# A gated three-branch decoder layer on one core: pools padded to 256 bytes, head outputs split by ScalarE and VectorE

## The chip, the core and the metric

The kernel runs on one core of a Trainium2 chip. Its engines are TensorE (matmuls, with the load of the stationary operand shown apart as PEld), VectorE (DVE), ScalarE (ACT), GpSimd (POOL) and SyncE (SP), which here only issues DMAs. The metric is the device time of one execution in microseconds, the median of three runs.

## The reference

One decoder layer on 512 tokens of width 1,024, in float32:

```
h = rmsnorm(x);  P = h @ w_in
A = gelu(g_rnn) * rg_lru(causal_conv4(x_rnn))            # 1024 wide
B = rmsnorm_per_head(diff_attention(dq, dk, dv)) * 0.8   # 4 heads of 128
C = forgetting_attention(fq, fk, fv, log_f)              # 8 heads of 64
m = sum_b sigmoid(gate_b) * (Y_b @ W_branch_b)           # Y_b = A, B, C
x = x + m @ w_out
x = x + geglu_with_causal_conv3(rmsnorm(x) @ ffn_up) @ ffn_down   # d_ff 2816
out = rmsnorm(x)
```

## The kernel before

**Arithmetic.** Every large matmul is done in three. Each float32 operand is split into a high part, rounded to TensorE's float32r, and a low part, the rest; then high x high, high x low and low x high are summed in PSUM. A split costs a copy or scaled copy on one engine (high) and a subtraction on another (low). `load_w` (L93) loads a weight tile on SP's DMA queue into `wr`, ScalarE writes `wh` (L101), VectorE `wl` (L102). `mm3` (L79) issues the three matmuls of each of 8 slices of the contraction, 24 for a tile of 512 columns; all of them are recorded at L77.

**Stages, in order of time.** Values of the diff heads (psv); then a list of units (L791 to L836): each unit is one attention head, `diff_head` (L439) or `fox_head` (L517), between whose pieces projections (psq, psk), the recurrent branch (psx, psg), the gates (psgt) and the branch products (psbr) are emitted as filler, by weights written out by hand. Then the output projection (pswo), the up projection with its convolution (psu), the down projection (psd). The order on each engine's queue is set when the program is scheduled, from this list.

**Head outputs.** A diff head ends with a scaled copy from PSUM into `yd` (L502); the four tiles are split much later by `ysplit` (L678), with ScalarE's copy (L682) and GpSimd's subtraction (L683), as an item of the unit of the first Fox head (`yds`, L797). Two Fox heads write the halves of one `yf` tile (L566, L567); the four tiles are split by the same helper in `end_attention` (L822). The recurrent branch's output `yr` goes through `ysplit` too. The branch products (`prod`, L655) read the parts.

**Space.** The pools lie one behind the other in each partition's bytes. Tiles are rounded up to 32 bytes. The constants end, and the page pool begins, at byte 23,840 = 93 x 256 + 32: 58 tiles of 2,048 bytes, which hold nearly everything 128x512, the parts of x and h2 that stream through TensorE among it. Behind it `wpool`: nine slots of 1,056 x 4 = 4,224 bytes, three each of `wr`, `wh` and `wl`; the three `wh` start at 160, 32 and 160 mod 256 and the three `wl` at 32, 160 and 32. Then the small tiles (`sm`, 3,008 bytes) and the 22 attention tiles of 2,048 bytes, at 96 mod 256, whose space takes ten pairs of `wo` and then of the FFN's activations (`act`, k < 10) later. Weight tiles take the three slots in turn.

**PSUM.** Four banks for the projections and products (`bank`, L67), four for attention (`abank`, L70). A projection's bank is free when VectorE has read it, as `xs` (L587) does for psx.

Of the kernel before, what the change touches and what calls it, by code (L numbers as in the profile page):

```python
# [24 lines left out]
NPG = 58  # L25
NAT = 22
NWARM = 9
NLAST = (2, 4)
LAM_INIT = 0.2
GELU_C = 0.7978845608028654  # L30
# [7 lines left out]
    COFF[_n] = _o  # L38
    _o += _w
NCOL = _o  # L40
ROFF = {"fbf": 0, "lam": 8}
NROW = 264

T_XR, T_GR, T_DQ, T_DK, T_FQ, T_FK, T_GT = 0, 8, 16, 20, 24, 28, 32

# [1 line left out]
def build(ctx, tc, A, out):  # L47
# [13 lines left out]
    def pg(name, dt=F32):  # L61
        return page.tile([128, 512], dt, name=name, tag="pg")

    def ag(name, dt=F32):
        return apool[0].tile([128, 512], dt, name=name, tag="at")
# [7 lines left out]
    def small(shape, name, bufs=None):  # L73
        return sm.tile(shape, F32, name=name, tag=name, bufs=bufs)
# [16 lines left out]
    hp = [False]  # L91

    def load_w(ap, n, parts=1):  # L93
        raw = wpool.tile([128, 1056], F32, name="wr", tag="wr")
        hi = wpool.tile([128, 1056], F32R, name="wh", tag="wh", bufs=3)
        lo = wpool.tile([128, 1056], F32R, name="wl", tag="wl", bufs=3)
        with tc.high_priority() if hp[0] else ExitStack():
            for p in range(parts):
                c = slice(n // parts * p, n // parts * (p + 1))
                nc.sync.dma_start(raw[:, c], ap[:, c])  # L100
                SC.copy(hi[:, c], raw[:, c])  # L101
                V.tensor_sub(lo[:, c], raw[:, c], hi[:, c])  # L102
        return hi, lo

    def load_wp(ap):

        raw = wpool.tile([128, 1056], F32, name="wr", tag="wr")
        nc.sync.dma_start(raw[:, :1024], ap)
        res = []
        for p in range(2):  # L110
            c = slice(512 * p, 512 * (p + 1))
            h = pg("wph", F32R)
            l = pg("wpl", F32R)
            SC.copy(h, raw[:, c])
            V.tensor_sub(l, raw[:, c], h)
            res.append((h, l))
        return res
# [39 lines left out]
    V.memset(epsc, EPS)  # L157
    pre = const.tile([128, 1], F32, name="pre")
    SC.activation(pre, epsc, AF.Exp)
    rows = const.tile([128, NROW], F32, name="rows")  # L160

    def col(n, j, w=1):
        return cols[:, COFF[n] + j:COFF[n] + j + w]
# [59 lines left out]
    nc.sync.dma_start(flip, A["flip"])  # L223
    flr = const.tile([128, 128], F32R, name="flr")
    V.tensor_copy(flr, flip)
    nc.sync.dma_start(rows, A["rows"].partition_broadcast(128))
    relb = const.tile([32, 4], F32, name="relb")
    nc.sync.dma_start(relb, A["rel_bias"])
    oh = ag("oh")[0:32, :]
# [19 lines left out]
    PE.matmul(bps[0:4, :], relb, oh, start=True, stop=True)  # L249
    bsb = ag("bsb")[0:4, :]  # L250
    V.tensor_copy(bsb, bps[0:4, :])
    bneg = const.tile([4, 128], F32, name="bneg")
    V.memset(bneg, NEG)
    bdr = dram.tile([4, 640], F32, name="bdr")
    nc.sync.dma_start(bdr[:, 0:512], bsb)
# [19 lines left out]
    def ev_fv(g):  # L275
        def ev(t, ps):
            p = pg("fv", F32R)

            pv = p.rearrange("p (u x d) -> p u x d", u=2, x=4)
            src = ps[:, 0:256].rearrange("p (u x d) -> p u x d", u=2, x=2)  # L280
            with tc.high_priority():
                for x in range(2):
                    h = pv[:, :, 3 * x, :]
                    l = pv[:, :, 1 + x, :]
                    SC.activation(h, src[:, :, x, :], AF.Copy, scale=rs1[:, t:t + 1])
                    V.scalar_tensor_tensor(l, src[:, :, x, :], rs1[:, t:t + 1], h, op0=MUL, op1=SUB)
            fv[t][g] = p
            if g == 0:
                V.scalar_tensor_tensor(flog[:, t, :], ps[:, 256:264], rs1[:, t:t + 1],
                                       rows[:, ROFF["fbf"]:ROFF["fbf"] + 8], op0=MUL, op1=ADD)  # L290
        return ev


# [13 lines left out]
        slabs.append(tl)  # L307


    lamw = rows[:, ROFF["lam"]:ROFF["lam"] + 256].rearrange("p (a b) -> p a b", a=4)  # L310
    lamp = ag("lamp")[:, 0:128].rearrange("p (a b) -> p a b", a=2)
    V.tensor_mul(lamp, lamw[:, 0::2, :], lamw[:, 1::2, :])
    lams = small([128, 2], "lams", 1)
    V.tensor_reduce(lams, lamp, axis=mybir.AxisListType.X, op=ADD)
    lame = small([128, 2], "lame", 1)
    SC.activation(lame, lams, AF.Exp)
# [122 lines left out]
    def diff_head(h, res):  # L439
        ws = []  # L440
        for i in range(NT):
            n = 128 * (i + 1)
            p = []
            nm = small([128, 2], "nm")
            mx = small([128, 2], "mx")
            sm_ = small([128, 2], "sum")
            for m in range(2):
                ps = scores(("d", h), m, i)
                sc = ag("sc")
                V.tensor_tensor_reduce(sc[:, :n], ps[:, :n], slabs[h][:, 512 - n:], 1.0, NEG, ADD, MAX,  # L450
                                       mx[:, m:m + 1])
                p.append(sc)
            V.tensor_scalar(nm, mx, -1.0, None, op0=MUL)
            for m in range(2):
                SC.activation(p[m][:, :n], p[m][:, :n], AF.Exp, bias=nm[:, m:m + 1], accum_out=sm_[:, m:m + 1])
            rc = small([128, 2], "rc")
            V.reciprocal(rc, sm_)
            V.tensor_mul(rc[:, 1:2], rc[:, 1:2], nlam)
            V.tensor_scalar(p[0][:, :n], p[0][:, :n], rc[:, 0:1], None, op0=MUL)
            V.scalar_tensor_tensor(p[0][:, :n], p[1][:, :n], rc[:, 1:2], p[0][:, :n], op0=MUL, op1=ADD)  # L460
            ws.append(p[0])
            yield
        yield "B"
        po = abank("pso")
        hs = slice(128 * h, 128 * (h + 1))

        def av(j):
            wh, wl = wt[j]
            c = slice(min(128 * j, 256), 512)
            for x, (a, b) in enumerate(((dvl[j][:, hs], wh), (dvh[j][:, hs], wl), (dvh[j][:, hs], wh))):  # L470
                mm(po[:, c], a, b[:, c], j == 0 and x == 0, j == NT - 1 and x == 2)

        wt = []
        for j in range(NT):
            wt.append(transposed(ws, j))
            if j:
                av(j - 1)
            if j % 2:
                yield
        av(NT - 1)  # L480
        o = ag("o")
        SC.copy(o, po)
        yield
        pt = abank("psq")
        for t in range(NT):
            PE.transpose(pt[:, 128 * t:128 * (t + 1)], o[:, 128 * t:128 * (t + 1)], ident)
        sq = ag("sq")
        so = small([128, NT], "so")
        for t in range(NT):
            c = slice(128 * t, 128 * (t + 1))  # L490
            SC.activation(sq[:, c], pt[:, c], AF.Square, accum_out=so[:, t:t + 1])
        rs = rsqrt_col(so, NT, "rso", 1.0 / 128)
        on = ag("on")
        for t in range(NT):
            c = slice(128 * t, 128 * (t + 1))
            V.tensor_scalar(on[:, c], pt[:, c], rs[:, t:t + 1], None, op0=MUL)
        yield
        pn = abank("psn")
        for t in range(NT):
            PE.transpose(pn[:, 128 * t:128 * (t + 1)], on[:, 128 * t:128 * (t + 1)], ident)  # L500
        y = pg("yd")
        SC.activation(y, pn, AF.Copy, scale=sg8)  # L502
        res.append(y)
        yield

    fo = {}
# [10 lines left out]
    def fox_head(hd, res):  # L517
# [48 lines left out]
        SC.copy(tmp[a], po[b])  # L566
        V.tensor_add(o[a], po[a], tmp[a])  # L567
        if m == 1:
            res.append(o)
        yield  # L570


# [105 lines left out]
    def ysplit(ys, name):  # L678
        for j in range(len(ys)):
            h = pg(name + "h", F32R)  # L680
            l = pg(name + "l", F32R)
            SC.copy(h, ys[j])  # L682
            G.tensor_sub(l, ys[j], h)  # L683
            ys[j] = (h, l)
# [62 lines left out]
    def do(f):  # L747
        return [(0.1, None, f)]
# [3 lines left out]
    def unit(gen, items):  # L752

        start = len(queue)
        queue.extend(items)
        plan.append((gen, start, len(queue)))
# [25 lines left out]
    def ckl(hd):  # L782
        return do(lambda: ck_load(hd))
# [3 lines left out]
    p1 = [f for c in range(0, 8, 2) for f in pi_(1, c)]  # L787
    vf = [(10, vload_t(A["wv_f0"], 4, 264), lambda w: vchunk_t(w, 4, 264, ev_fv(0))),
          (10, vload_t(A["wv_f1"], 4, 256), lambda w: vchunk_t(w, 4, 256, ev_fv(1)))]
    yds, yrs = do(lambda: ysplit(yd, "yd")), do(lambda: ysplit(yr, "yr"))  # L790
    unit(None, qi("d", 0) + ri(0))  # L791
    unit(DH(0, yd), qi("d", 1)[:1] + ri(1)[:1] + qi("d", 1)[1:] + ri(1)[1:] + re((0, 1)) + ri(2))
    unit(DH(1, yd), qi("d", 2)[:1] + gi(1, 1) + ri(3)[:1] + qi("d", 2)[1:] + ri(3)[1:])
    unit(DH(2, yd), gi(1, 0) + qi("f", 0)[:1] + qi("d", 3) + ri(4) + gi(1, 3))
    unit(DH(3, yd), vf[1:] + re((2, 3)) + vf[:1] + gi(1, 2) + gi(1, 4) + do(fox_prep) + qi("f", 0)[1:] + gi(1, 5)
         + gi(1, 6) + gi(1, 7) + qi("f", 1)[:1] + ckl(0))
    unit(F(0, yf), ri(5) + yds + ckl(1) + re((4, 5)))  # L797
    unit(F(1, yf), qi("f", 1)[1:] + ckl(2) + ri(6) + qi("f", 2)[:1])
    unit(F(2, yf), p1[2:] + p1[:1] + ri(7)[:1] + p1[1:2] + ri(7)[1:] + ckl(3))
    unit(F(3, yf), gi(0, 1) + gi(0, 0) + re((6, 7)) + yrs + ckl(4) + qi("f", 2)[1:] + gi(0, 2) + pi_(0, 1))  # L800
# [5 lines left out]
    wo = [None] * KD  # L806

    def wo_load(k):
        raw = wpool.tile([128, 1056], F32, name="wr", tag="wr")
        nc.sync.dma_start(raw[:, :1024], A["w_out"][128 * k:128 * (k + 1), :])  # L810
        hl = []
        for hf in range(2):
            al = ag if k < 5 else pg
            h = al("woh", F32R)
            l = al("wol", F32R)
            SC.copy(h, raw[:, 512 * hf:512 * (hf + 1)])
            V.tensor_sub(l, raw[:, 512 * hf:512 * (hf + 1)], h)
            hl.append((h, l))
        wo[k] = hl

    def end_attention():
        ysplit(yf, "yf")  # L822
        att_ctx.close()
        apool[0] = ctx.enter_context(tc.tile_pool(name="fpool", bufs=NAT))

# [67 lines left out]
                V.scalar_tensor_tensor(h2l[k][:, ts_], src, col("g2", k), h2h[k][:, ts_], op0=MUL, op1=SUB)  # L893


    fwh = const.tile([128, 88], F32, name="fwh")
    for j in range(3):
        V.tensor_scalar(fwh[:, 22 * j:22 * (j + 1)], col("fw", 44 * j + 22, 22), 0.5, None, op0=MUL)
    V.tensor_scalar(fwh[:, 66:88], col("fb", 22, 22), 0.5, None, op0=MUL)
# [166 lines left out]
```

## Time and profile before

| | |
|---|---|
| median of 3 runs | 949.76 us (948.43 to 950.57) |
| profiled execution | 949.56 us, its span 947.7 us |
| mean granted TensorE clock | 0.996 |
| busy: PE, DVE, ACT, POOL | 99%, 67%, 51%, 12% |
| matmuls | 4,363 |

The span runs from the first to the last instruction; 1.8 us of the profiled execution lie around it. A matmul's own duration (about 0.39 us at 512 columns) includes its way through the array, which the next one overlaps: what it costs is the time from its start to the next start. PEclk is the granted clock as a share of full speed (2.4 GHz); its lower level is 0.5.

### The profile page before, as it was taken

How to read it: one execution, taken by the hardware profiler on the slowest of the kernel's cores; microseconds unless marked ns; L12 is line 12 of the kernel's file. 1: busy time of each engine (PE TensorE's matmuls, PEld its weight loads, DVE VectorE, ACT ScalarE, POOL GpSimd, SP SyncE). 2: the span in 40 equal slices, each digit the busy share in tenths (PEclk: the TensorE clock that was granted, in tenths of full speed). 3: DMA queues.
4: the chain of work that ended last, by engine and by line, in shares of the span. 5: the costliest groups of instructions: out<-in, count | busy, mean ns of one | idle time of the engine just before them, and what ended most of it. 6: DMA issues, size and time to landing. Idle time of an engine off the chain costs nothing.

```text
span 947.7 us, 11817 instructions
## 1 busy us (share of the span) xinstructions
PE 934.7 (99%) x4363; PEld 770.7 (81%) x4363; DVE 631.7 (67%) x1207; ACT 486.6 (51%) x839; POOL 112.4 (12%) x85
## 2 busy tenths in 40 slices
PE   9999999999998999999999999999999999999997
PEld 6788888998886887888888889888888888888885
DVE  5779787777669889755566634877677677633323
ACT  7668776855474775434453344544444444422212
POOL 0022210200133253221210000000000000000000
PEclk9999999999999999999999999999999999999999
DMA  9622222232231323223253600323223222334112
GB/s 320 194 80 87 95 73 68 68 112 76 98 106 58 104 67 112 85 82 101 67 200 110 207 16 1 112 91 109 90 89 99 102 89 90 112 105 140 45 67 89
DMA packets 31433, 95.14 MB, mean 100 GB/s; under 512 B 3680, under 2 KB 5220, under 8 KB 31376
## 3 DMA queue, kind: packets, MB, share of 16 engines
q1 hardware_dynamic: 30800, 93.35, 29.2%
q10 hardware_dynamic: 576, 1.05, 0.3%
q8 instruction: 34, 0.56, 0.2%
q14 instruction: 23, 0.19, 0.1%
HBM read 92.26 MB, written 2.12 MB: 100 GB/s over the span
## 4 chain that ended last, share of the span: by engine, by line
PE 95%; DVE 3%; issue 1%; DMA 0%; ACT 0%; SPq 0%; POOLq 0%; POOL 0%
PE psu L77 26%; PE psgt L77 13%; PE psd L77 12%; PE psbr L77 9%; PE psg L77 6%; PE psv L77 5%; PE psx L77 5%; PE pswo L77 5%; PE psq L77 4%; PE psk L77 4%; PE pss L77 2%; PE pso L77 2%; PE pst L429 1%; DVE hh L637 1%; DVE gr L638 1%
## 5 line engine op out<-in xcount | busy, mean ns | idle before, releaser
L101 ACT CAST wh<-wr 128x1024 fp32r<-128x1024 f32 (+2 forms) x143 | 146.4, 1024 | 157.0 <-PE psu L77 55.3
L102 DVE TENSOR_TENSOR wl<-wr,wh 128x1024 fp32r<-128x1024 f32 (+2 forms) x143 | 174.1, 1217 | 75.3 <-ACT wh L101 66.7
L77 PE MATMUL psu<-h2l,wh 128*128 128x512 f32 (+1 forms) x360 | 136.9, 384 | 0.0
L77 PE MATMUL psu<-h2h,wh 128*128 128x512 f32 (+1 forms) x360 | 136.9, 383 | 0.0
L77 PE MATMUL psu<-h2h,wl 128*128 128x512 f32 (+1 forms) x360 | 87.2, 384 | 0.0
L77 PEld LDWEIGHTS psu<-h2l,wh 128*128 128x128 f32 x360 | 67.8, 188 | 14.0
L77 PEld LDWEIGHTS psu<-h2h,wh 128*128 128x128 f32 x360 | 67.8, 188 | 13.8
L77 PEld LDWEIGHTS psu<-h2h,wl 128*128 128x128 f32 x360 | 65.8, 188 | 14.4
L77 PE MATMUL psgt<-xh,wh 128*128 128x512 f32 x192 | 76.6, 399 | 0.0
L77 PE MATMUL psgt<-xl,wh 128*128 128x512 f32 x192 | 76.2, 397 | 0.0
L77 PE MATMUL psd<-wh,actl 128*128 128x512 f32 x128 | 50.2, 393 | 0.0
L77 PE MATMUL psd<-wl,acth 128*128 128x512 f32 x128 | 50.1, 391 | 0.0
L77 PE MATMUL psd<-wh,acth 128*128 128x512 f32 x128 | 49.9, 392 | 0.0
L77 PE MATMUL psgt<-xh,wl 128*128 128x512 f32 x192 | 49.1, 395 | 0.0
L864 POOL TENSOR_TENSOR rs3y<-rs3y,mhalf 128x1 f32<-128x1 f32 x4 | 2.2, 551 | 364.5 <-DVE rs3y L863 364.5
L77 PEld LDWEIGHTS psgt<-xh,wl 128*128 128x128 f32 x192 | 35.7, 188 | 8.1
L77 PEld LDWEIGHTS psgt<-xh,wh 128*128 128x128 f32 x192 | 36.1, 188 | 7.5
L77 PEld LDWEIGHTS psgt<-xl,wh 128*128 128x128 f32 x192 | 36.1, 188 | 7.5
L926 DVE SCALAR_TENSOR_TENSOR u<-gq,u 128x512 f32<-128x512 f32 x22 | 15.2, 692 | 34.1 <-ACT gq L925 34.1
L651 DVE TENSOR_TENSOR z<-psgt,rsb 128x512 f32<-128x512 f32 x24 | 16.5, 688 | 31.1 <-PE psgt L77 31.1
L906 DVE SCALAR_TENSOR_TENSOR u<-psu,cols,u 128x511 f32<-128x511 f32 (+1 forms) x44 | 32.9, 748 | 6.1 <-ACT u L903 5.3
L123 ACT CAST acth<-u 128x512 fp32r<-128x512 f32 x22 | 13.7, 621 | 43.5 <-DVE u L927 43.5
(288 smaller groups left out, 2179.6 us busy)
## 6 DMA issues: line engine op xcount, KB each, us to landing
wr<-w_t_in SPq DMA_DIRECT2D x56, 512.0 KB, 3.3
wr<-up_t_in SPq DMA_DIRECT2D x44, 512.0 KB, 3.3
wr<-dn_t_in SPq DMA_DIRECT2D x22, 512.0 KB, 3.4
wr<-br_r_in SPq DMA_DIRECT2D x8, 512.0 KB, 3.4
wr<-w_out_in SPq DMA_DIRECT2D x8, 512.0 KB, 3.9
xraw<-xT_in SPq DMA_DIRECT2D x8, 256.0 KB, 6.0
wr<-wv_d_in SPq DMA_DIRECT2D x8, 256.0 KB, 5.4
xt<-x_in SPq DMA_DIRECT2D x8, 256.0 KB, 5.4
```

The costliest lines, as they stand in the source:

```text
L77: PE.matmul(ps, a, b, start=start, stop=stop)
L101: SC.copy(hi[:, c], raw[:, c])
L102: V.tensor_sub(lo[:, c], raw[:, c], hi[:, c])
L123: SC.copy(h, src)
L429: PE.transpose(ps[:, 128 * i:128 * (i + 1)], ws[i][:, 128 * j:128 * (j + 1)], ident)
L637: V.tensor_tensor_scan(hh, a, xc, 0.0, op0=MUL, op1=ADD)
L638: V.scalar_tensor_tensor(gr, gr, 0.5, hh, op0=MUL, op1=MUL)
L651: V.tensor_mul(z, ps, rsb)
L864: G.tensor_tensor(y, y, mhalf[:, 0:1], op=ALU.pow)
L906: V.scalar_tensor_tensor(u[:, s:], ps[:, :512 - s], w[j], u[:, s:], op0=MUL, op1=ADD)
L926: V.scalar_tensor_tensor(ug, q, 1.0, ug, op0=ADD, op1=MUL)
```

## The change

Two things are done. First, sizes are changed so that each pool's start and slots are multiples of 256 bytes: the weight slots get 1,088 columns instead of 1,056 (4,352 bytes, 17 x 256); the constants lose the vectors for lambda (`rows`, from 264 columns to 8) and `bneg`, both now in one attention tile `lamr`, and `fwh` grows from 88 to 144 columns: 1,024 + 512 - 224 = 1,312 bytes less, so the page pool begins at 22,528 = 88 x 256. `lams` grows by 64 bytes, so the small tiles take 3,072. The load of `rows` becomes two DMAs. Second, `diff_head` writes the high part straight from PSUM (ScalarE) and the low part from PSUM (VectorE); `fox_head` calls `split` (L119: ScalarE copy, VectorE subtraction) on each finished `yf`; the calls of `ysplit` for yd and yf go. The one for yr stays.

```diff
+WCOL = 1088
...
-ROFF = {"fbf": 0, "lam": 8}
-NROW = 264
+NFB = 8
...
-        raw = wpool.tile([128, 1056], F32, name="wr", tag="wr")
-        hi = wpool.tile([128, 1056], F32R, name="wh", tag="wh", bufs=3)
-        lo = wpool.tile([128, 1056], F32R, name="wl", tag="wl", bufs=3)
+        raw = wpool.tile([128, WCOL], F32, name="wr", tag="wr")
+        hi = wpool.tile([128, WCOL], F32R, name="wh", tag="wh", bufs=3)
+        lo = wpool.tile([128, WCOL], F32R, name="wl", tag="wl", bufs=3)
...
-    rows = const.tile([128, NROW], F32, name="rows")
+    rows = const.tile([128, NFB], F32, name="rows")
...
-    nc.sync.dma_start(rows, A["rows"].partition_broadcast(128))
+    nc.sync.dma_start(rows, A["rows"][0:NFB].partition_broadcast(128))
+    lamr = ag("lamr")
+    nc.sync.dma_start(lamr[:, 0:256], A["rows"][NFB:NFB + 256].partition_broadcast(128))
...
-    bneg = const.tile([4, 128], F32, name="bneg")
+    bneg = lamr[0:4, 384:512]
...
-    lamw = rows[:, ROFF["lam"]:ROFF["lam"] + 256].rearrange("p (a b) -> p a b", a=4)
-    lamp = ag("lamp")[:, 0:128].rearrange("p (a b) -> p a b", a=2)
+    lamw = lamr[:, 0:256].rearrange("p (a b) -> p a b", a=4)
+    lamp = lamr[:, 256:384].rearrange("p (a b) -> p a b", a=2)
     V.tensor_mul(lamp, lamw[:, 0::2, :], lamw[:, 1::2, :])
-    lams = small([128, 2], "lams", 1)
+    lams = small([128, 24], "lams", 1)[:, 0:2]
...
-        y = pg("yd")
-        SC.activation(y, pn, AF.Copy, scale=sg8)
-        res.append(y)
+        h = pg("ydh", F32R)
+        l = pg("ydl", F32R)
+        SC.activation(h, pn, AF.Copy, scale=sg8)
+        V.scalar_tensor_tensor(l, pn, sg8, h, op0=MUL, op1=SUB)
+        res.append((h, l))
...
         if m == 1:
-            res.append(o)
+            res.append(split(o, "yf"))
...
-    yds, yrs = do(lambda: ysplit(yd, "yd")), do(lambda: ysplit(yr, "yr"))
+    yrs = do(lambda: ysplit(yr, "yr"))
...
-    unit(F(0, yf), ri(5) + yds + ckl(1) + re((4, 5)))
+    unit(F(0, yf), ri(5) + ckl(1) + re((4, 5)))
...
     def end_attention():
-        ysplit(yf, "yf")
...
-    fwh = const.tile([128, 88], F32, name="fwh")
+    fwh = const.tile([128, 144], F32, name="fwh")
```

## Rows read from the trace of the kernel before

**Rows 1.** The page: busy shares (part 1), and the chain that ended last (part 4).

```profile
PE 934.7 (99%) x4363; PEld 770.7 (81%) x4363; DVE 631.7 (67%) x1207; ACT 486.6 (51%) x839; POOL 112.4 (12%) x85
...
PE 95%; DVE 3%; issue 1%; DMA 0%; ACT 0%; SPq 0%; POOLq 0%; POOL 0%
```

**Rows 2.** The chain in order of time: start, length, what, and matmuls in it.

```profile
505.54 22.15 PE psbr L77 x96
...
574.49 5.50 PE psu L77 x46
580.86 239.11 PE psu L77 x1082
819.97 115.79 PE psd L77 x504
```

**Rows 3.** Timeline of TensorE, up projection, two weight tiles: start, duration, what.

```profile
658.90 0.40 PE L77 MATMUL psu<-h2h,wh 128*128 128x512 f32 x1
...
662.40 0.40 PE L77 MATMUL psu<-h2l,wh 128*128 128x512 f32 x1
662.64 2.02 PE L77 MATMUL psu<-h2h,wl 128*128 128x512 f32 x8
664.50 0.39 PE L77 MATMUL psu<-h2h,wh 128*128 128x512 f32 x1
...
667.90 0.40 PE L77 MATMUL psu<-h2l,wh 128*128 128x512 f32 x1
```

**Rows 4.** The same view of the down projection's last tiles, all in pages.

```profile
922.89 0.39 PE L77 MATMUL psd<-wpl,acth 128*128 128x512 f32 x1
...
926.97 0.39 PE L77 MATMUL psd<-wpl,acth 128*128 128x512 f32 x1
```

**Rows 5.** Lines L682, L683: count, duration ns min/median/max, first and last start.

```profile
L683 POOL TENSOR_TENSOR ydl<-yd,ydh x4: 1742/2097/2213, 280.2 to 286.5; 128x512 fp32r<-128x512 f32 x4
L683 POOL TENSOR_TENSOR yfl<-yf,yfh x4: 1287/1295/2282, 471.7 to 476.5; 128x512 fp32r<-128x512 f32 x4
...
L682 ACT CAST ydh<-yd x4: 617/637/637, 279.5 to 281.5; 128x512 fp32r<-128x512 f32 x4
```

**Rows 6.** Lines L244 and L124 on VectorE, the forms nearest to the new ones.

```profile
L244 DVE SCALAR_TENSOR_TENSOR dvl<-psv,rs,dvh x4: 729/744/747, 25.9 to 30.9; 128x512 fp32r<-128x512 f32 x4
...
L124 DVE TENSOR_TENSOR actl<-u,acth x22: 680/692/693, 601.6 to 826.3; 128x512 fp32r<-128x512 f32 x22
```

**Rows 7.** TensorE's stall (timeline), then two stretches: busy us by engine, PEclk.

```profile
293.13 0.50 PE L77 MATMUL psbr<-ydh,wh 128*128 128x512 f32 x1 [3.38 <-DVE xs L587]
...
280.00:293.10 13.10, 9.75 (x46) 7.58 (x44) 12.97 (x11) 6.20 (x12) 10.84 (x6) 1.00 0.22 71
293.10:306.00 12.90, 12.87 (x52) 10.53 (x53) 12.26 (x38) 7.45 (x15) 1.29 (x1) 0.87 0.25 83
```

**Rows 8.** VectorE's groups from 279 to 293.2 us; then those lines over the span.

```profile
L637 DVE TENSOR_TENSOR_SCAN hh<-a,xc 128x512 f32<-128x512 f32 x2 | 3.4, 1752 | 0.0
L638 DVE SCALAR_TENSOR_TENSOR gr<-gr,hh 128x512 f32<-128x512 f32 x2 | 2.8, 1433 | 0.0
L410 DVE TENSOR_TENSOR kl<-kf,kd 64x512 fp32r<-64x512 f32 x2 | 2.4, 1200 | 0.0
...
L637 DVE TENSOR_TENSOR_SCAN hh<-a,xc x8: 1198/1240/2330, 82.8 to 349.7; 128x512 f32<-128x512 f32 x8
L638 DVE SCALAR_TENSOR_TENSOR gr<-gr,hh x8: 684/906/1745, 84.0 to 354.1; 128x512 f32<-128x512 f32 x8
L410 DVE TENSOR_TENSOR kl<-kf,kd x16: 674/689/1709, 45.0 to 383.5; 64x512 fp32r<-64x512 f32 x16
```

**Rows 9.** Line L226, the load of rows on SP's queue.

```profile
L226 SPq DMA_DIRECT2D rows<-rows_in x1: 328/328/328, 19.8 to 19.8; - x1
```

**Rows 10.** Timeline of TensorE at the lower clock, behind the stall.

```profile
295.46 1.91 PE L77 MATMUL psbr<-ydh,wl 128*128 128x512 f32 x4
297.17 0.41 PE L429 MATMUL pst<-ident,sc 128*128 128x128 f32 x1
```

More of the change, by code (lines that the diff above doesn't have):

```diff
@@ L105, in load_wp @@
     def load_wp(ap):
-        raw = wpool.tile([128, 1056], F32, name="wr", tag="wr")
+        raw = wpool.tile([128, WCOL], F32, name="wr", tag="wr")
         nc.sync.dma_start(raw[:, :1024], ap)
@@ L289, in ev @@
                 V.scalar_tensor_tensor(flog[:, t, :], ps[:, 256:264], rs1[:, t:t + 1],
-                                       rows[:, ROFF["fbf"]:ROFF["fbf"] + 8], op0=MUL, op1=ADD)
+                                       rows, op0=MUL, op1=ADD)
         return ev
@@ L808, in wo_load @@
     def wo_load(k):
-        raw = wpool.tile([128, 1056], F32, name="wr", tag="wr")
+        raw = wpool.tile([128, WCOL], F32, name="wr", tag="wr")
         nc.sync.dma_start(raw[:, :1024], A["w_out"][128 * k:128 * (k + 1), :])
```

## The prediction

> **What bounds the kernel now.** I read the page's first and fourth part first. TensorE is busy 99% of a span of 947.7 us and carries 95% of the chain that ended last [rows 1]. So three things can shorten the kernel: fewer stalls of TensorE, a shorter step from one matmul to the next, or the clock. The second is nearly everything, and I read it from the chain in order of time, where a piece divided by its count is the mean step: 22.15 us for 96 psbr is 230.7 ns, 115.79 for 504 psd 229.7 [rows 2]. The 1,082 psu in 239.11 us hold 98 of 256 columns; these take 119.6 ns each (5.50 us for 46), which leaves 231.0 ns for the 984 of 512 columns [rows 2]. In the mean, 230.7.
>
> That step isn't one number, though, and this is what the reader should see next. In the timeline of TensorE in the up projection, sixteen starts on one weight tile (664.50 to 667.90, 15 steps) lie 226.7 ns apart; those on the tile before it (658.90 to 662.40) 233.3 ns [rows 3]. The work is the same; the weight buffer is not. The three wh buffers start at 160, 32 and 160 mod 256 bytes, since their slot of 4,224 bytes is 16.5 x 256; the page tiles that stream against them start at 32; the fast tile is the one whose buffer starts at 32. The same floor stands at the end, where both operands are page tiles: 18 steps from 922.89 to 926.97 take 4.08 us, 226.7 ns each [rows 4]. So where the stationary and the moving tile start at the same place mod 256, the matmuls settle at 226.7 ns, and elsewhere some 3 to 7 ns above. I call this the lock.
>
> **The change part by part.** *Padding, the largest term.* By the sizes of the tiles the constants shrink by 1,312 bytes, and every large tile of every pool then starts at 0 mod 256. All pairs of operands become equal ones. Counted from the loops outside the attention heads, 3,584 matmuls have 512 columns: 96 for the first values, 56 tiles x 24, 384 psbr, 192 pswo, 984 psu, 528 psd and 56 small ones. At 230.7 now [rows 2] and 226.7 after [rows 3, 4] each saves 4.0 ns: 3,584 x 4.0 = 14.3 us. Bounds: the most, if all of them stood at 233.3 today as the slow tile does, is 3,584 x 6.6 = 23.7; the least, if 0 against 0 doesn't lock as 32 against 32 does, is nothing. A loss would need equal tiles whose steps stay above 230.7, and on page against page I find none. I take 14, and not the upper bound, because the mean of the pieces is a measured one and a run needs some steps to settle: the eight wl steps behind the slow tile, 32 against 32 as well, still take (664.50 - 662.64)/8 = 232.5 ns [rows 3].
>
> Rows 3 speak for two readers of SBUF that get in each other's way. The Trainium skill ("TensorE: Matmul & The Clock Gate", Part 2: What happens when you issue a matmul) speaks against that: weight load and matmul have independent read ports, and loading the next weights takes nothing from the running matmul. By that rule where the tiles start couldn't matter, and this term would be 0; the trace doesn't agree, with 226.7 and 233.3 ns side by side [rows 3].
>
> *The splits of yd.* Four subtractions on GpSimd (2,097 ns in the median, the last one begun at 286.5 us) and four ScalarE copies (637 ns) go [rows 5]. ScalarE's scaled copy out of PSUM stays and now writes the high part. VectorE gains one scalar_tensor_tensor of 128x512 out of PSUM for each head. The nearest row is the same form in dvl, 744 ns [rows 6]: 3.0 us, three of the four long before 280 us, where TensorE doesn't wait, and one near 279.
>
> This falls on the one real stall. TensorE waits 3.38 us for a bank that VectorE's xs frees [rows 7], and from 280 to 293.1 us VectorE is busy for 12.97 of 13.10 us [rows 7]: there it is the bound. Part of its work is drawn out: beside a busy GpSimd the hh take 1,752 ns, the gr 1,433 and the kl 1,200, two of each, against least durations of 1,198, 684 and 674 of the same lines [rows 8]; L411's two kl are taken as like L410's. That is 2 x 554 + 2 x 749 + 4 x 526 = 4.7 us. GpSimd is busy for 10.84 us of the stretch [rows 7], some 8.2 of it with ydl (4 x 2.04, nearest their median) [rows 5]; by that share 3.5 us of the 4.7 go, and 0.74 come back as the fourth yd split. So the stall shrinks by 2.7 us. It cost clock too: behind it the granted clock falls to its lower level (1.2 GHz), a mean of 0.87 over 12.9 us [rows 7], so 12.9 x 0.13 = 1.7 us of full speed are lost, and I let them come back. Sum 4.4; bounds 0 (GpSimd's other work stretches VectorE as before) and 3.38 + 1.7 = 5.1. I take 4, near the upper end, since ydl is three quarters of what runs beside VectorE there. Next to be late is xs itself, behind gr and kl in VectorE's order.
>
> *The splits of yf.* The same subtraction on VectorE, 692 ns by its nearest form, actl [rows 6], 2.8 us in all, one behind each odd Fox head; ScalarE's copies move with them. The products that read them begin at 505.54 us [rows 2], the last yfl began at 476.5 [rows 5]: nothing while these 29 us stand. Were VectorE the bound where one falls, that one would cost 0.7.
>
> *Small things.* One more DMA issue behind one of 328 ns at 19.8 us on SP's queue [rows 9], with the bias loads behind it and matmuls of the first values beside it: nothing, at most its 0.3 us. Wider slots and the tile lamr only use room. A faster TensorE catches up with VectorE from 280 to 320 us, where VectorE is the bound: 40 us hold 40/0.2307 = 173 steps, and 173 x 4.0 ns = 0.7 us of the gain is at stake; I give back 0.5.
>
> Sum, against the profiled execution of 949.56 us (its span and 1.8 us around it): 949.6 - 14 - 4 + 0.5 = 932. The median of the runs, 949.76, lies 0.2 above, which changes nothing: **932 us**. As long as it is this case, it reaches from 922 (both upper bounds) to 941 (half of both terms).
>
> **The rivals.** *The floor falls too* (0.15). 226.7 ns may itself be the price of tiles that start at 32. At the lower clock four matmuls of 512 columns go from 295.46 to 297.17, 427.5 ns each [rows 10]; half of that is 213.75. So at the full clock 13 ns per matmul are lost that at half speed are hidden, as if one more piece of an operand had to be read, and aligned tiles could save that piece. Price: 3,584 x 12.95 = 46 us, 886; if half of it comes, 909. Against it: what the lock asks for is equal starts, and moving both tiles by 32 bytes changes nothing between them. The Trainium skill ("TensorE: Matmul & The Clock Gate", Wait — 56ns, not 53.3ns?) has a fixed cost of about 2.5 ns per matmul at the full clock, by which this rival would be worth an estimated 39 us; no run here shows it.
>
> *The padding does nothing* (0.20). The slow buffers may be slow for something else that turns with three buffers. Only the splits are left: 949.6 - 4 = 945.5, from 944 to 950. Against it: the floor of rows 4 is that of rows 3, with other tiles. By the rule of independent ports weighed above, this is what should come.
>
> *Slower: the page tiles run out* (0.12). Each finished diff head holds two page tiles instead of one until the products near 286 us. Counted from the code, at 250 us 16 parts of x, 8 gates, 8 fv, 8 parts of dv, 3 yd and some 9 tiles of the recurrent branch live, 52 of 58; three more make 55. If the next tile due for reuse is then still read, rgw's load, which SP issues in order, waits for it, the weight loads queue behind, and TensorE runs dry. A dry spell costs what the one of rows 7 did, 3.4 + 1.7 = 5.1 us. Beside an idle padding two of them decide it: 949.6 - 4 + 10 = 956; beside the lock it would take five. Against it: three tiles are still spare.
>
> **How the numbers follow.** Forecast 0.50, falling floor 0.15, idle padding 0.20, page tiles 0.12, anything else 0.03. A measurement of this kernel tells about 0.2% from no change, 947.9 to 951.7 us. Faster than that: 0.50 + 0.15 + 0.12 of the idle case = 0.77. Within it: 0.07 of the idle case and 0.02 of the page tiles, 0.09. Slower: the remaining 0.14. The range runs from 900, which takes in the weaker half of the falling floor (0.07), to 951, which takes in the forecast and the idle case whole (0.70) and a little of the rest: about 8 in 10.
>
> **What would show it.** Lock: steps of 226.7 ns on all three weight buffers, the long psu piece of the chain near 239.1 - 984 x 0.0043 = 235 us, psd's near 114. Falling floor: steps of 214 to 220 ns. Idle padding: two tiles in three still near 233. Splits: no GpSimd subtraction for yd and yf, gr and kl near 0.7 us around 285 us, TensorE's wait there under 1 us and the granted clock at 1.00 behind it. I am wrong if equal starts at 0 behave unlike equal starts at 32, or if new waits on VectorE or SP appear in the attention heads.

## The result, and the profile after

The changed kernel takes 937.50 us (median of 4 runs, 936.32 to 938.80) against 950.16 us for the kernel before, a ratio of 0.987 with an interval of 0.9849 to 0.9892: faster by 12.7 us, where 18 were forecast. Measured again later, it took 936.35 us (934.95 to 936.52), 0.9852 [0.9837, 0.9867].

The profiled execution is one of 938.8 us, with a span of 937.0 us. The eight times of this kernel stand in two groups, six from 934.95 to 936.52 and two above 938.5: the profile taken with the second measurement (span 934.6 us) has 22.08 us in its first piece of 96 psv, the one shown here 24.32 us, because the clock rose later in it, which has nothing to do with the change.

The page of after, busy shares (part 1) and chain (part 4), answering to [rows 1]:

```profile
PE 925.1 (99%) x4363; PEld 771.6 (82%) x4363; DVE 633.8 (68%) x1215; ACT 482.7 (52%) x835; POOL 95.9 (10%) x77
...
PE 96%; DVE 2%; issue 1%; ACT 0%; DMA 0%; POOLq 0%; POOL 0%; SPq 0%; ACTq 0%
```

The bound is the same and only shorter: TensorE 99% busy, 96% of the chain. GpSimd lost 8 instructions and 16.5 us. The chain of after in order of time (start, length, what, matmuls), answering to [rows 2]:

```profile
501.62 21.76 PE psbr L77 x96
...
569.68 5.51 PE psu L77 x46
...
576.07 234.82 PE psu L77 x1082
810.89 114.25 PE psd L77 x504
```

The long psu piece is 4.29 us shorter, psd 1.54 and psbr 0.39: 22.15 us for 96 became 21.76, 226.7 ns each. The short psu piece, 5.50 and 5.51 us, holds matmuls of 256 columns and did not move. TensorE's timeline of after in the up projection, the end of one weight tile, a whole one, and the start of a third (start, duration, what), answering to [rows 3], and of the down projection's page tiles, answering to [rows 4]:

```profile
647.75 0.39 PE L77 MATMUL psu<-h2l,wh 128*128 128x512 f32 x1
...
650.92 0.39 PE L77 MATMUL psu<-h2l,wh 128*128 128x512 f32 x1
651.15 1.98 PE L77 MATMUL psu<-h2h,wl 128*128 128x512 f32 x8
652.96 0.39 PE L77 MATMUL psu<-h2h,wh 128*128 128x512 f32 x1
...
656.36 0.39 PE L77 MATMUL psu<-h2l,wh 128*128 128x512 f32 x1
656.59 1.98 PE L77 MATMUL psu<-h2h,wl 128*128 128x512 f32 x8
658.40 0.39 PE L77 MATMUL psu<-h2h,wh 128*128 128x512 f32 x1
...
908.64 0.39 PE L77 MATMUL psd<-wph,actl 128*128 128x512 f32 x1
...
916.80 0.39 PE L77 MATMUL psd<-wph,actl 128*128 128x512 f32 x1
```

From 650.92 to 656.36 lie 24 steps, 5.44 us, 226.7 ns each, with the eight wl steps among them; from 647.75 to 650.92 on the tile before it are 14, 226.4 ns by the rounded ends. Slow tiles are gone. The page tiles at the end run as before, 36 steps in 8.16 us.

VectorE's new subtractions and the head of the stretch where TensorE used to stall, answering to [rows 5 to 8]: the lines L506 and L124; TensorE's waits in the timeline there; two stretches (busy us and count by engine, then PEclk, DMA share, GB/s); and VectorE's groups from 279 to 293.2 us:

```profile
L506 DVE SCALAR_TENSOR_TENSOR ydl<-psn,sg,ydh x4: 742/744/746, 140.4 to 279.2; 128x512 fp32r<-128x512 f32 x4
...
L124 DVE TENSOR_TENSOR yfl<-yf,yfh x4: 672/692/693, 330.2 to 478.7; 128x512 fp32r<-128x512 f32 x4
...
292.23 0.30 PE L431 MATMUL pst<-ident,sc 128*128 128x128 f32 x1 [0.53 <-DVE mx L535]
293.35 0.39 PE L77 MATMUL pso<-wtl,fv 128*128 128x256 f32 x1 [0.82 <-DVE wtl L438]
...
280.00:291.30 11.30, 11.30 (x54) 9.46 (x54) 11.21 (x13) 5.03 (x8) 2.88 (x2) 1.00 0.27 96
291.30:306.00 14.70, 13.35 (x61) 10.46 (x60) 14.57 (x44) 9.37 (x19) 1.29 (x1) 1.00 0.26 89
...
L412 DVE TENSOR_TENSOR kl<-kf,kd 64x512 fp32r<-64x512 f32 x2 | 2.5, 1242 | 0.0
L641 DVE TENSOR_TENSOR_SCAN hh<-a,xc 128x512 f32<-128x512 f32 x2 | 2.4, 1214 | 0.0
L413 DVE TENSOR_TENSOR kl<-kf,kd 64x512 fp32r<-64x512 f32 x2 | 1.4, 686 | 0.0
L642 DVE SCALAR_TENSOR_TENSOR gr<-gr,hh 128x512 f32<-128x512 f32 x2 | 1.3, 674 | 0.0
```

The wait of 3.38 us for xs has become waits of 0.53 and 0.82 us, and the clock stays at 1.00. GpSimd's 10.84 us there are 2.88; in the mean, hh went from 1,752 ns to 1,214 and gr from 1,433 to 674. But this row, in TensorE's waits (line, what it waited for: us in total, times, longest), was not there before, and the clock now falls behind it (second fence: two stretches, the same columns as above):

```profile
PE psbr L77 <- ACT yrh L686: 2.2, 1, 2.2
```

```profile
343.00:355.00 12.00, 10.22 (x53) 8.32 (x51) 9.29 (x19) 11.63 (x19) 2.08 (x1) 1.00 0.21 67
355.00:368.00 13.00, 12.54 (x53) 10.28 (x54) 11.12 (x27) 9.02 (x19) 12.47 (x9) 0.87 0.16 60
```

TensorE waits near 353 us for the recurrent branch's first high part, which ScalarE had finished at 345.0 us in the kernel before and now finishes at 355.4. The stall that was removed at 290 us has a smaller one in its place, 60 us later, with the same drop of the clock behind it, a mean of 0.87 over 13 us.

### The profile page after: what moved, and what is told of

The parts are those of the page before. It is cut to its first block, busy times and chain, and to the rows that moved or that the text cites. A ratio compares the mean times of both kernels' runs of the same rounds, so it can differ in the third digit from the quotient of the medians.

```text
span 937.0 us, 11825 instructions
## 1 busy us (share of the span) xinstructions
PE 925.1 (99%) x4363; PEld 771.6 (82%) x4363; DVE 633.8 (68%) x1215; ACT 482.7 (52%) x835; POOL 95.9 (10%) x77
## 4 chain that ended last, share of the span: by engine, by line
PE 96%; DVE 2%; issue 1%; ACT 0%; DMA 0%; POOLq 0%; POOL 0%; SPq 0%; ACTq 0%
PE psu L77 26%; PE psgt L77 14%; PE psd L77 12%; PE psbr L77 9%; PE psg L77 6%; PE psv L77 5%; PE psk L77 5%; PE psx L77 5%; PE pswo L77 5%; PE psq L77 4%; PE pss L77 2%; PE pso L77 2%; PE pst L431 1%; DVE wl L102 0%; PE psh L891 0%
## 5 line engine op out<-in xcount | busy, mean ns | idle before, releaser
L77 PEld LDWEIGHTS psu<-h2h,wh 128*128 128x128 f32 x360 | 67.7, 188 | 12.7
L437 ACT CAST wth<-pst 128x512 fp32r<-128x512 f32 (+3 forms) x48 | 19.6, 423 | 28.8 <-PE pst L431 27.1
```

What stands on the lines that cost most here:

```text
L77: PE.matmul(ps, a, b, start=start, stop=stop)
L437: SC.copy(h[:, 128 * j:], ps[:, 128 * j:])
```

## The experiments

Two questions were open: what the padding is worth and why, and where the gain of the splits went. Times of each kernel stand against the kernel before on the same chip in the same job (950.56, 949.72, 950.54 and 950.25 us in the four jobs).

**The padding alone, the splits alone.** The first kernel is after with the split edits taken out, the second is before with only these put in (the calls of `ysplit` come back or go with them and aren't shown):

```diff
-        h = pg("ydh", F32R)
-        l = pg("ydl", F32R)
-        SC.activation(h, pn, AF.Copy, scale=sg8)
-        V.scalar_tensor_tensor(l, pn, sg8, h, op0=MUL, op1=SUB)
-        res.append((h, l))
+        y = pg("yd")
+        SC.activation(y, pn, AF.Copy, scale=sg8)
+        res.append(y)
...
-            res.append(split(o, "yf"))
+            res.append(o)
```

> The padding alone, head outputs split as before. Lock: steps of 226.7 ns, some 12 us below before (12.4 us of excess over 226.7 ns go in the trace of the changed kernel): 938 us; if the splits brought the 4 us I forecast, this one is 4 us slower than the changed kernel, 941.5. Idle padding: 950.

> The splits alone, pools as before. My step: 4 us below before, 945.5, and no wait above 1 us near 290 us. Rival: the wait moves to the split of yr (TensorE waits 2.2 us for yrh at 353 us in the changed kernel), then 949 to 950, no difference.

Padding alone: 939.26 us (938.70 to 939.38), 0.9879 [0.9865, 0.9894], 11.3 us less. Splits alone: 947.75 us (947.34 to 949.84), 0.9975 [0.9961, 0.9988], 2.8 us less. The two add up to 14.1, and what is measured for both is 12.7 and, again, 14.2. Both kernels missed what was expected of them by 1 to 2 us: the padding was put at 938, the splits at 945.5 or, if the wait only moved, at 949 to 950. TensorE's waits tell the splits' part cleanly: with the padding alone the row of before stands (3.4 us for xs), with the splits alone the row of after.

```profile
PE psbr L77 <- DVE xs L589: 3.4, 1, 3.4
```

```profile
PE psbr L77 <- ACT yrh L684: 2.2, 1, 2.2
```

**Which starts are fast.** A kernel with nothing but matmuls of 512 columns, in groups of 32, on tiles whose starts are shifted in steps of 32 bytes:

```python
def run(name, mo, so, n=512, cols=128, reps=REP, step=1):
    ps = psm.tile([128, 512], F32, name=name, tag="mm")
    for r in range(reps):
        m = mv[:, mo + 512 * (r % 2):mo + 512 * (r % 2) + n]
        s = sw[:, so + 128 * (r % 8):so + 128 * (r % 8) + cols]
        PE.matmul(ps[0:cols, 0:n], s, m, start=True, stop=True)
    return ps
```

> Only matmuls of 128x512 in float32r, no layer is computed. For each pair of starts (moving and stationary tile at 0, 32, ... 224 mod 256) 32 matmuls follow each other; the letters a to h in a result's name are the starts in steps of 32 bytes, m for moving, s for stationary. Theory of the lock (the difference of the two starts decides): the eight equal pairs run at 226.7 ns, pairs that differ by 128 near 232.4, by 64 or 96 near 230, whatever the starts are. Theory of the boundary (a start at 0 mod 128 or 256 is what counts): only the pairs with both at 0 are at 226.7 or below. Idle: all pairs alike. Then 96, 64 and 32 stationary columns instead of 128: if the 13.3 ns above 512/2.4 come from reading the stationary tile, 223, 220 and 217 ns; if they are a fixed cost, 226.7 in all three. 384 and 256 moving columns: 173 and 120 ns in both.

Its timeline (start, length of a group of 32, what; the letters behind m and s are the starts of the moving and the stationary tile, a = 0, b = 32 bytes, to h = 224):

```profile
24.59 7.42 PE L39 MATMUL masa<-mv,sw 128*128 128x512 f32 x32
31.85 7.62 PE L39 MATMUL masb<-mv,sw 128*128 128x512 f32 x32
...
54.26 7.59 PE L39 MATMUL mase<-mv,sw 128*128 128x512 f32 x32
...
69.15 7.49 PE L39 MATMUL masg<-mv,sw 128*128 128x512 f32 x32
...
91.42 7.46 PE L39 MATMUL mbsb<-mv,sw 128*128 128x512 f32 x32
...
291.80 7.42 PE L39 MATMUL mese<-mv,sw 128*128 128x512 f32 x32
...
499.56 7.53 PE L39 MATMUL colsnsix<-mv,sw 128*96 128x512 f32 x32
...
514.29 7.57 PE L39 MATMUL colstwo<-mv,sw 128*32 128x512 f32 x32
```

The last matmul of a group lasts 0.39 us, so masa's step is (7.42 - 0.39)/31 = 226.8 ns. Taken over the second half of each group, from the starts of the single matmuls, the 64 pairs fall on one list that depends only on the distance from the moving to the stationary start mod 256 (medians; 63 of them lie within 0.4 ns of it, and mesa, at distance 128, takes 233.4):

| distance, bytes | 0 | 32 | 64 | 96 | 128 | 160 | 192 | 224 |
|---|---|---|---|---|---|---|---|---|
| ns per matmul | 226.7 | 233.3 | 233.3 | 234.1 | 232.0 | 233.2 | 228.7 | 233.3 |

So the lock is real, it needs equal starts and not aligned ones (mbsb and mese settle at the same 226.7 as masa), and its floor doesn't move. Distances of 64 and 96 bytes had been expected near 230 and are slower. With 96 or 32 stationary columns at equal starts the step is not shorter but longer, 230.0 and 231.7 ns: the 13.3 ns above 512 columns at 2.4 GHz don't shrink with the stationary tile's columns, although a load of 32 takes 109 ns and one of 128 takes 188. With 384 and 256 columns the steps were 173.3 and 120.0 ns, 13.3 above the same rate each time. By the Trainium skill ("TensorE: Matmul & The Clock Gate", Part 2: What happens when you issue a matmul) weight load and matmul read through independent ports; by that, starts couldn't matter, and these runs don't agree.

**Equal starts at 32 bytes.** After, with one constant widened so that every large tile moves by 32 bytes:

```diff
-    rows = const.tile([128, NFB], F32, name="rows")
+    rows = const.tile([128, 16], F32, name="rows")[:, 0:NFB]
```

> The changed kernel with every pool shifted by 32 bytes: one tile of constants is 64 bytes instead of 32, so all large tiles start at 32 mod 256 instead of 0. Lock: nothing changes, 937.5 us and steps of 226.7 ns. Boundary: the gain goes, 950 us.

936.64 us (934.98 to 937.03), 0.985 [0.9833, 0.9866], the time of after. "Multiples of 256 bytes" is one way to get equal starts and has no merit of its own.

**All weight tiles 128 bytes off.** After, with a pool of 128 bytes ahead of the weight pool:

```diff
+    gap = ctx.enter_context(tc.tile_pool(name="gap", bufs=1))
+    gap.tile([128, 32], F32, name="gap")
     wpool = ctx.enter_context(tc.tile_pool(name="wpool", bufs=3))
...
-    lams = small([128, 24], "lams", 1)[:, 0:2]
+    lams = small([128, 56], "lams", 1)[:, 0:2]
```

> The kernel after with all nine weight tiles 128 bytes off the page tiles (0 mod 256). Theory of equal starts: before, two of three weight buffers stood 128 bytes off and cost 12.4 us in the trace against after; here three of three do, so 12.4 x 3/2 = 18.6 us more than after, 937.5 + 18.6 = 956 (954 to 958), with every step on the weight tiles near 232 ns, the 232.0 that the map gave at 128 bytes, and the late products on page tiles still at 226.7. Rival (the turn of three buffers or the slot's length sets the slow step, and tiles at whole 128 bytes are good enough): the time of after, 937 to 939.

951.28 us (950.97 to 954.44), 1.0022 [1.0012, 1.0031], 13.8 above after: unequal starts take back more than the 11.3 us of the padding, though not the 18.6 that I had put on it. The chain of this kernel, in order of time:

```profile
505.43 22.40 PE psbr L79 x96
...
580.51 240.28 PE psu L79 x1082
820.80 116.61 PE psd L79 x504
```

psbr is at 233.3 ns. I scaled by buffers, two of three to three of three, but steps should have been counted. By the starts of single matmuls (steps below 250 ns, floor 226.67), with the tiles' distances:

| kernel | distance 0 | 128 | 192 | 64 | above the floor, us |
|---|---|---|---|---|---|
| before | 1,572 of 229.1 ns | 1,564 of 232.6 | 276 of 230.4 | 163 of 231.6 | 15.0 |
| after | 3,561 of 227.4 | | | 8 | 2.5 |
| weights 128 off | 516 of 228.9 | 3,061 of 232.6 | | 8 | 19.3 |

The steps cost 19.3 - 2.5 = 16.8 us more than in after, within 2 us of the 18.6. The steps of 250 ns and more, which hold waits and the lower clock, cost 4.2 us less in this profile than in the one of after, so that the spans, 949.3 and 937.0, differ by 12.3. In the kernel before, nearly half of the steps (first column) stood at distance 0 and still took 2.4 ns above the floor, as the wl steps of [rows 3] do. They lie between slow tiles; that they settle late for this is argued, since in the map only one of the eight equal groups (mbsb, 230.6 ns over its first eight steps) began slow.

**The map in steps of 4 bytes.** The same kernel of matmuls, distances 0 to 252, then with one stationary tile all the time, with each used twice, and with bf16 tiles:

```python
for i in range(64):
    run("f" + LET[i // 8] + LET[i % 8], 0, i)
run("onest", 0, 0, one=True)
run("halfst", 0, 0, half=True)
run("small", 0, 0, bf=True)
run("smalldiff", 0, 32, bf=True)
```

> This kernel leaves the whole layer out and runs only matmuls of 512 columns in groups of 32, each group with the stationary tiles starting at another distance from the moving ones: 0 to 252 bytes in steps of 4 (names fxy, distance 4*(8x+y) bytes with a=0 to h=7), then with one stationary tile all the time (onest), with each used twice in a row (halfst), and with bf16 operands at distance 0 (small) and 64 bytes (smalldiff). Theory of equal starts: 226.7 ns at distance 0 alone or within a few bytes of it, 229 to 234 ns at the others, none below 226.6; bf16 loads are half as long, so at 64 bytes bf16 loses less than the 6.6 ns of the float32r tiles. Rival (a lower floor exists): some distance that is no multiple of 32 gives 214 to 224 ns. Rival (the 13.3 ns above 512 columns at 2.4 GHz are the load of a new stationary tile): onest falls to 214 to 220 ns, halfst half way; if they stay at 226.7, the load isn't their cause.

Timeline, groups of 32 as above:

```profile
25.76 7.42 PE L45 MATMUL faa<-mv,sw 128*128 128x512 f32 x32
...
211.89 7.42 PE L45 MATMUL fdb<-mv,sw 128*128 128x512 f32 x32
...
330.15 7.74 PE L45 MATMUL ffb<-mv,sw 128*128 128x512 f32 x32
...
501.11 7.44 PE L45 MATMUL onest<-mv,sw 128*128 128x512 f32 x32
508.38 7.42 PE L45 MATMUL halfst<-mv,sw 128*128 128x512 f32 x32
515.64 7.08 PE L45 MATMUL small<-bm,bs 128*128 128x512 bf16 x32
522.55 7.07 PE L45 MATMUL smalldiff<-bm,bs 128*128 128x512 bf16 x32
```

No distance is below 226.6 ns, so the falling floor is out. Distance 0 isn't alone: 100 (fdb), 120, 132, 144, 156, 228 and 252 bytes settle at 226.7 too; the slowest, 164 (ffb), takes 236.9. One stationary tile all the time (it is still loaded 32 times, 187 ns each) changes nothing (226.6), so the 13.3 ns aren't the change of tile either; whether they go when nothing is loaded at all was not run. With bf16 the step is 215.8 ns at 0 and at 64 bytes, where float32r takes 226.7 and 233.3; other distances were not run with bf16. Its loads take 98 ns in place of 188, so the type and the length of the load aren't told apart. The Trainium skill ("TensorE: Matmul & The Clock Gate", Wait — 56ns, not 53.3ns?) has about 2.5 ns of fixed cost per matmul; 215.8 against 512/2.4 = 213.3 ns agrees for bf16, and 226.7 does not for float32r.

**The recurrent branch's splits, each as it comes.** After, with the same treatment for the third set of heads' outputs, to remove the new wait (the late call goes with it):

```diff
-            yr[c] = gr
+            yr[c] = split(gr, "yr")
```

> The kernel after with the outputs of the recurrent branch split too as each comes, the high part by ScalarE and the low part by VectorE, in the place of eight splits in a row ahead of their first product. Theory (the splits' gain was eaten by TensorE's wait of 2.2 us for the first high part of the recurrent branch near 355 us and by the clock that fell behind it, some 1.7 us): that wait goes, the clock stays at 1.00 from 355 to 368 us, and the time is 937.5 - 3.9 = 933.6 (932 to 935). Rival (VectorE, full from 280 to 320 us and near 350, is the bound there, and eight more subtractions of 0.7 us come back as a wait for VectorE): 936 to 941 with a wait for gr, xs or yrl in its place.

937.33 us (936.15 to 938.71), 0.9868 [0.985, 0.9886]: no gain, as the rival said. The wait for yrh went, and this one came in its place, near 291 us:

```profile
PE pss L77 <- DVE mx L535: 2.1, 1, 2.1
```

The chain there runs through VectorE's kl, yrl and gr; VectorE is busy for 12.85 of the 13 us from 280 to 293, and the clock falls behind the wait (0.95 and 0.91 in the two stretches to 306 us).

**The diff heads' splits alone**, with the padding; the Fox heads' outputs are split late again and by GpSimd, all four in a row:

```diff
-            res.append(split(o, "yf"))
+            res.append(o)
...
     def end_attention():
+        ysplit(yf, "yf")
```

> The kernel after with the Fox heads' outputs split late and by GpSimd as before; the diff heads' are split as each comes. It tells which of the two moves made the wait near 355 us. If it is the diff heads' (the yrh follow VectorE's gr and the order of the queues changed from 250 us on): the wait of 2.2 us for yrh stands here too, 937 to 938.5. If it is the Fox heads' (their subtraction on VectorE or their copy on ScalarE stands ahead of the split): the wait near 355 us goes and the time is 933 to 935.

935.70 us (934.74 to 936.46), 0.985 [0.9835, 0.9865]. The same kernel and after once more, both on one chip:

> Padding and the diff heads' splits as they come, the Fox heads' late and by GpSimd: the earlier such kernel again, in more rounds. Theory (the Fox heads' early splits cost what they push back, the splits of the recurrent branch): 1 to 2.5 us below the kernel after of the same chip, 935 to 936. Rival (their times lie within each other's spread): within 0.7 us of the kernel after.

> The kernel after once more, beside the next two on the same chip, since the differences asked for are of two tenths of a per cent. Every theory: 937.5, 936 to 938.8, with the wait of 2.2 us for the recurrent branch's first high part near 353 us; what it shows is the spread of this kernel, in which the granted clock falls behind that wait in some executions and in others not.

934.76 (934.62 to 936.88), 0.9844 [0.9829, 0.9858], against 936.35 for after. Over eight runs each the medians are 935.0 and 936.4: the kernel without the Fox heads' edit is 1.4 us faster, though the ranges overlap. What tells more is the trace: the wait of 2.2 us for yrh is gone, though three short ones for VectorE (0.52, 0.37 and 0.71 us from 347 to 355 us) stand near its place, the clock stays at 1.00, and these splits begin at 338 us in place of 355 (count, duration ns min/median/max, first and last start; here, then in after):

```profile
L686 ACT CAST yrh<-gr x8: 603/619/624, 338.4 to 349.7; 128x512 fp32r<-128x512 f32 x8
```

```profile
L686 ACT CAST yrh<-gr x8: 605/617/624, 354.8 to 362.2; 128x512 fp32r<-128x512 f32 x8
```

So it is the Fox heads' split that pushed them back. The traces also show by what way. The matmuls of the last recurrent block (psx) end near 311 us in both kernels, but VectorE's xs, which reads them and begins that block's gates, stands in another place of VectorE's queue (timeline; the kernel with the diff heads' splits alone, then after's second profile, where it comes behind the first Fox pair's split):

```profile
312.40 0.68 DVE L591 TENSOR_TENSOR xs<-psx,rsb 128x512 f32<-128x512 f32 x1
```

```profile
327.92 0.69 DVE L124 TENSOR_TENSOR yfl<-yf,yfh 128x512 fp32r<-128x512 f32 x1
328.62 0.69 DVE L591 TENSOR_TENSOR xs<-psx,rsb 128x512 f32<-128x512 f32 x1
```

All eight profiles with the Fox heads' split inside the head have this xs from 327.9 to 334.5 us, the four without it from 312.4 to 318.0. The block's work on ScalarE follows, and the eight yrh stand behind it: from 306 to 343 us ScalarE is busy for 19.66 us in after's second profile and for 28.61 with the diff heads' splits alone.

Two more kernels tried to say what does it. One asks for six of the eight splits ahead of the first gate of that unit (its new place in the unit and the helper's new argument aren't shown); in the other the Fox heads' low parts are GpSimd's:

```diff
-    yrs = do(lambda: ysplit(yr, "yr"))
+    yrs = [do(lambda: ysplit(yr, "yr", range(0, 6))), do(lambda: ysplit(yr, "yr", range(6, 8)))]
...
-            res.append(split(o, "yf"))
+            h = pg("yfh", F32R)
+            l = pg("yfl", F32R)
+            SC.copy(h, o)
+            G.tensor_sub(l, o, h)
+            res.append((h, l))
```

> The kernel after with six of the eight splits of the recurrent branch's outputs asked for at the head of the unit of Fox head 3, ahead of its first gate, and only the last two where all eight stood; ScalarE and GpSimd do them as before. Theory (the wait near 353 us is one of order: the eight splits are asked for last and stand on ScalarE behind two loads of function tables; nothing lacks time): the wait of 2.2 us for yrh goes and the time falls to that of the kernel with the diff heads' splits alone, 935 to 936. Rival (ScalarE or GpSimd hasn't the time there): the wait stays or another of 1 to 2 us for yrh or yrl takes its place, 937 to 939.

> The kernel after with the Fox heads' outputs still split as each comes, the high part by ScalarE, but the low part by GpSimd in the place of VectorE. It tells which of the two moved the recurrent branch's splits behind ScalarE's table loads near 353 us. If it is VectorE's subtraction: the wait for yrh goes and the time is that of the kernel with the diff heads' splits alone, 934.6 to 936. If it is ScalarE's copy, or that the split is asked for inside the head at all: the wait of 2.2 us for yrh stands and the time is that of the kernel after, 936 to 938.6.

Asked for early: 938.51 us (937.95 to 939.93), 0.9876 [0.986, 0.9892], the slowest of these, against my theory. TensorE now waits 2.21 us until 355.07 for a maximum of VectorE's, which stands in its queue behind a weight split (wl) and so behind ScalarE's wh at 351.42; the chain from TensorE's next wait leads back through the same pieces of ScalarE:

```profile
348.98 1.28 ACT L636
...
350.91 0.51 ACT yrh L686
351.42 0.95 ACT wh L101
352.37 1.04 ACT yrh L686 x2
...
353.43 1.28 ACT L539
```

Two loads of function tables, 1.28 us each, with splits and a weight copy between them, stand in ScalarE's queue. ScalarE is busy for 11.94 of the 12 us from 343 to 355, as the rival had it, and for 3.85 of them with the diff heads' splits alone: the last block's gates have been pushed into this stretch. Just before it ScalarE stood idle for 3.79 us, while the inputs of the six splits had been finished since 286.3 us and the splits stood behind the gates in its queue (timeline):

```profile
342.34 0.63 ACT L613 ACTIVATE gq<-gq 128x512 f32<-128x512 f32 x1 [3.79 <-POOL gq L612]
```

So the time was there, and the order of ScalarE's queue kept the splits from it; asking for them earlier in the list didn't change that order enough. Low parts on GpSimd: 936.48 us (935.21 to 938.80), 0.9863 [0.984, 0.9885], the wait of 2.2 us for yrh stands. So VectorE's 0.7 us each don't do it, and xs is late all the same (327.9 us). What is left is ScalarE's copy or that the split is asked for inside the head, by which the order of the queues differs; these two were not told apart, and why the new order puts xs behind the Fox pair is not shown.

## Why the prediction came out as it did

*Direction and range* came out: 937.5 lies in 900 to 951. The time was 5.5 us above the 932 forecast and within the 922 to 941 that the likeliest case had for itself: the mechanism was right, and two terms were off in size.

*Padding.* The mechanism held as it was told: steps of 226.7 ns on all weight tiles, the long psu piece at 234.82 (235 forecast), psd at 114.25 (114), equal starts at 0 as good as at 32. The term was 14.3 us and measured 11.3 alone. The step that failed is "each saves 4.0 ns": after still has 2.5 us above the floor, nearly all in the attention stages, where shorter matmuls stand between those of 512 columns (2.3 of the 2.5 lie in the last step before one of these and in the first eight behind it), and I had put every matmul at the floor. With the 15.0 of before that makes 12.4 by the trace, 3.5 ns each. The rest is in the clock: with the padding alone the stall near 290 us is still 3.4 us, and the clock was at 0.89 and 0.84 in the stretches around it against 1.00 and 0.87 before, 1.8 us of full speed more.

*The splits of yd* were sized well: 4 us forecast, and 939.26 - 935.0 = 4.3 between padding alone and padding with the diff heads' splits (2.7 and 4.5 by the two measurements, each against the kernel before of its own chip). Some of it is the clock that padding alone had lost there. The rows it named are there: gr at 674 ns, three kl of four near 0.69 (one still 1.81), TensorE's waits near 290 us 0.53 and 0.82, clock 1.00.

*The splits of yf* were the mis-sized term: 0 forecast, some 1.4 us lost (936.4 - 935.0). I priced VectorE's subtraction and looked only for the reader of yf, 29 us later. The run with GpSimd shows that VectorE's part was indeed nothing; but with the edit the last recurrent block's xs stands 16 us later in VectorE's queue (312.4 and 328.6 us), the recurrent branch's splits begin 14 to 16 us later (338.4; 352.5 and 354.8), behind two table loads, and TensorE waits for them. Most of the price seems to be the clock behind that wait. The kernel at 32 bytes has the same wait of 2.2 us at the same time as after's second profile, keeps the clock at 1.00, and its profiled execution took 934.98 us; after's second profile has 0.91 and 0.95 there, 1.7 us of full speed, and took 936.36; the one with the diff heads' splits alone took 934.74. These are single executions. The sentence in the prediction that new waits in the attention heads would show me wrong named VectorE and SP; the queue that TensorE waited for was ScalarE's, 52% busy over the span and 97% in those 12 us, with work that VectorE had begun late.

*The give-back* of 0.5 us for VectorE can't be told from the runs' spread. With the measured terms the sum from the 950.56 us of that job is 950.56 - 11.3 - 4.3 + 1.4 = 936.4, as it must be, since the terms are differences of these medians.

*Rivals.* The falling floor is out: with float32r tiles of 512 columns no distance and no number of stationary columns goes below 226.6 ns. The idle padding is out: -11.3 us alone. The page tiles didn't stop TensorE: none of its waits is for a transfer. The load of the last rgw, which that rival named, does come later with the Fox heads' early splits (326.8 to 332.7 us against 301.2 to 307.4); whether page tiles set this order, no run tells.

*Left open:* what the lock is. Two readers in each other's way fit the dependence on the distance, but that was only argued, and the list of fast distances in steps of 4 bytes has no rule that I can see. Open too is why the clock fell behind the wait at 353 us in both profiles of after (0.87; 0.91 and 0.95) and not in the one at 32 bytes, whose wait is the same (2.2 us; 1.00 there).

## What to carry to other kernels

With float32r operands, let the stationary and the moving tile of a matmul start at the same place mod 256 bytes: a slot size that is no multiple of 256 in a rotating pool can cost 5 to 7 ns of 227 on the matmuls whose tiles then start apart (3.5 in the mean here), and the chain's pieces divided by their counts show it. The distances other than 0 that were fast in the map of 4-byte steps were not tried in a layer. A step moved earlier has to be costed on the queue it is moved into, at the time it is moved to, for those who stand behind it, not only for who reads its result; and where a scheduler sets the order of the queues, it can move work that the edit doesn't touch. When a stall is taken out, look for the next in the same kind of stretch: here it came back smaller, 60 us later, with the same fall of the clock.

## What was not expected of the hardware

In the map of 32-byte steps the step of a float32r matmul of 512 columns depends on the distance of its two operands' starts mod 256 and, in 63 of 64 pairs, on nothing else of their place: 226.7 ns at 0, 228.7 at 192, 232.0 to 234.1 at the other multiples of 32. Above the rate of one column per cycle at 2.4 GHz there are 13.3 ns per float32r matmul, the same for 512, 384 and 256 columns, and 2.5 ns per bf16 matmul of 512 columns, which is the same at 0 and 64 bytes. With fewer stationary columns (96 to 32) the step grew by 3.3 to 5.0 ns.
